# MLP down products with activation tiles in the array and 512-wide weight rows moving

## The chip, the cores and the metric

The kernel runs on one core of a Trainium2 chip. The metric is device time in microseconds for one execution of the whole program; the kernel before takes 2779.71 us (median of 3 runs, 2779.48 to 2797.15).

## What is computed

A two-layer encoder trunk over 256 tokens of width 2048. Layer 0 mixes tokens by sparse attention, layer 1 by an RWKV-7 recurrence; after each comes the MLP that this case is about:

```python
hff = rms_norm(x) * (1 + sc2) + sh2
x = x + g2 * (jnp.square(jax.nn.relu(hff @ mlp_w1[i])) @ mlp_w2[i])
```

`mlp_w1` is 2048 x 8192 and `mlp_w2` 8192 x 2048, float32. A last RMS norm ends the program.

## The kernel before

Activations stand transposed on the chip: `x[f]` is a 128 x 256 tile, 128 features by 256 tokens, 16 tiles in all. Every float32 operand of a product is split into a high part in fp32r and the remainder, and a product is the sum of three matmuls: high times high, high times low, low times high (`acc3`, L179 to L186).

The MLP (`mlp`, L341) goes through the hidden width in four blocks `b` of 2048. For a block, 16 calls of `up(b, f)` (L365) each load one 128 x 2048 slab of `mlp_w1`, run 48 matmuls into one PSUM bank and turn the result into a hidden tile `hid[b, f]` of 128 features by 256 tokens, with its high part in the first 256 columns and its low part in the next 256. Then 16 calls of `down(b, f)` (L382) each load one slab of `mlp_w2`, run 48 matmuls over the 16 hidden tiles into one bank and add the bank into `y[f]` (L389; block 0 copies it, L387). In block 3 each `down` ends by multiplying `y[f]` with its gate and adding it into `x[f]` (L391), then squares `x[f]` for the next norm (`tally`, L290), and GpSimd adds the squares into `ssq` (L292). Two `up` calls of the next block are issued ahead of the down products (`AHEAD_UP`); block 3 has none.

In both kinds of product the weight is the stationary operand: a matmul loads a 128 x 128 weight tile and moves 256 token columns (258 in `up`).

Weights come in pieces of 128 x 512 (`Weights`, L85): SyncE issues a 256 KB load into a ring of 10 raw buffers, ScalarE casts the high part (L92), and the low part is a subtraction (L94), on VectorE for pieces 0 and 1 of a slab and on GpSimd for pieces 2 and 3. High and low parts stand in a ring of 10 pieces; a piece's buffers are free when the last matmul that reads them is done. A slab is four pieces. Beside this the first MLP carries the adaLN rows of the coming layers: at 0.8 rows for each slab, a 1 MB load (L222) and one multiply-and-sum on VectorE (L224); the second MLP carries 0.2 for each slab.

PSUM has two banks each of kinds `d` and `m` and one each of `a` and `b` (asked for as `c`). The products of the MLP take banks in the turn d, c, m (`dense`, L188). The order of instructions on each engine is settled when the program is built, by a scheduler that simulates the engines; each engine then works through its list in order.

Of the kernel before, what the change touches and what calls it, by code (L numbers as in the profile page):

```python
# [7 lines left out]
F32 = mybir.dt.float32  # L8
# [4 lines left out]
OP = mybir.AluOpType  # L13
# [3 lines left out]
P = 128  # L17
D = 2048
S = 256
NS = S + 2  # L20
NF = D // P
# [56 lines left out]
def ada_by_row(layer, part, j):  # L78
    return layer == 1 or part == 5 or (part > 1 and j == 2)
# [22 lines left out]
class Trunk:  # L102
# [238 lines left out]
    def mlp(s, layer):  # L341
        nc = s.nc
        s.kinds = "dcm"


        h = []
        ts = [s.tp.tile([P, 2 * NS], F32R, name="h", bufs=NF) for i in range(NF)]
        rb = s.tp.tile([P, S], F32, name="rb")
        for i, t in enumerate(ts):
            sh = s.m(layer, 3, i).to_broadcast([P, NS - S])  # L350
            nc.gpsimd.tensor_copy(t[:, S:NS], sh)
            nc.gpsimd.tensor_tensor(t[:, NS + S:], sh, t[:, S:NS].bitcast(F32), op=OP.subtract)
        for i, t in enumerate(ts):
            sc = s.m(layer, 4, i)
            nc.scalar.activation(t[:, :S], s.x[i], AF.Copy, scale=sc)
            nc.vector.scalar_tensor_tensor(t[:, NS:NS + S], s.x[i], sc, t[:, :S].bitcast(F32),  # L356
                                           op0=OP.mult, op1=OP.subtract)
            h.append(t)
        for i in range(NF):
            s.tally(i)  # L360
        cols = [k * P for k in range(16)]
        y = [s.tp.tile([P, S], F32, name=f"y{f}") for f in range(NF)]
        hid = {}

        def up(b, f):  # L365
            w = s.wload(s.io["mlp_w1"][layer, b * 16 + f])
            s.ada_due()
            p = s.dense(w, h, cols)
            if b == f == 0:
                nc.scalar.copy(rb, s.rms(D, [s.ssq, s.lsq]))  # L370
            u, r, q = s.B(), s.B(), s.B()
            c = s.small(1)
            nc.scalar.copy(c, p[:, S:S + 1])
            nc.vector.tensor_tensor(u, p[:, :S], rb, op=OP.mult)  # L374
            nc.scalar.activation(r, u, AF.Relu, bias=c)  # L375
            nc.vector.tensor_tensor(q, r, r, op=OP.mult)  # L376
            t = s.O() if 1 < f < 2 + NO else s.A(F32R)
            nc.scalar.activation(t[:, :S], r, AF.Square)
            nc.vector.tensor_tensor(t[:, S:], q, t[:, :S].bitcast(F32), op=OP.subtract)
            hid[b, f] = t  # L380

        def down(b, f):  # L382
            w = s.wload(s.io["mlp_w2"][layer, b, f])
            s.ada_due()
            p = s.dense(w, [hid[b, k] for k in range(16)], cols)
            if b == 0:
                nc.scalar.copy(y[f], p)  # L387
            else:
                nc.vector.tensor_tensor(y[f], p, y[f], op=OP.add)  # L389
            if b == 3:  # L390
                nc.vector.scalar_tensor_tensor(s.x[f], y[f], s.m(layer, 5, f), s.x[f], op0=OP.mult, op1=OP.add)  # L391
                s.tally(f)


        for b in range(4):
            for f in range(AHEAD_UP if b else 0, 16):
                up(b, f)
            for f in range(AHEAD_UP if b < 3 else 0):
                up(b + 1, f)
            for f in range(16):  # L400
                down(b, f)

    def out_group(s, name, layer, block, g, movs, first=0):

# [769 lines left out]
def layout(inputs):  # L1174
    import numpy as np
    g = {k: np.asarray(a) for k, a in inputs.items()}
    f = np.float32
    ct = np.ascontiguousarray
    vec = lambda a: a.reshape(-1, P).T

    def tiles(w, rows, cols):

        n = w.shape[1] // cols
        return ct(w.reshape(rows, P, n, cols).transpose(2, 1, 0, 3)).reshape(n, P, rows * cols)

    a = {}
    a["x"] = ct(g["x"][0].T.reshape(NF, P, S).transpose(1, 0, 2)).reshape(P, NF * S)
    a["positions"] = ct(g["positions"].reshape(-1))
    mu = g["b_mu"][0]
    vs = dict(c=g["c"], final_g=g["final_g"], w0=g["b_w0"], a0=g["b_a0"], k_k=g["b_k_k"], k_a=g["b_k_a"],  # L1190
              gn_g=g["b_gn_g"], gn_b=g["b_gn_b"], r_k=g["b_r_k"], q_norm_g=g["a_q_norm_g"],
              kv_norm_g=g["a_kv_norm_g"], ada_b0=g["ada_b"][0], ada_b1=g["ada_b"][1],
              **{f"mu{i}": mu[i] for i in range(6)})
    a["vec"] = ct(np.concatenate([vec(vs[n]) for n in VEC], 1))
    a["cst"], a["csd"] = constants()
    a["kidx_ln"] = ct(np.stack([g["a_kidx_ln_g"][0], g["a_kidx_ln_b"][0]], 1))
    aw = g["ada_w"]
    rows = aw.transpose(0, 2, 1).reshape(2, 24, 4, P, D)
    cols = aw.reshape(2, 4, 4, P, 24, 512).transpose(0, 4, 1, 3, 2, 5).reshape(2, 24, 4, P, D)
    a["ada_w"] = np.stack([np.stack([(rows if ada_by_row(l, b // 4, b % 4) else cols)[l, b] for b in range(24)])  # L1200
                           for l in range(2)])
    a["c"] = ct(g["c"].reshape(-1))
    a["mlp_w1"] = np.stack([tiles(w, 16, P) for w in g["mlp_w1"]])
    a["mlp_w2"] = np.stack([np.stack([tiles(w[b * 2048:(b + 1) * 2048], 16, P) for b in range(4)])
                            for w in g["mlp_w2"]])
    wi = g["a_w_in"][0]
    a["a_w_in"] = ct(wi[:, :896].reshape(8, 2, P, 896).transpose(0, 2, 1, 3)).reshape(8, P, 1792)
    a["a_w_in_idx"] = tiles(wi[:, 784:912], 16, P)[0]
    a["a_w_qidx"] = tiles(g["a_w_qidx"][0], 4, 512)
    uq = g["a_w_uq"][0].reshape(4, P, 16, 192)  # L1210
    uk = g["a_w_uk"][0].reshape(2, P, 16, P)
    out = []
    for b in range(4):
        hs = range(b * 4, b * 4 + 4)
        parts = [uq[k, :, h, :128] for h in hs for k in range(4)]
        parts += [np.concatenate([uq[k, :, h, 128:], uq[k, :, h + 1, 128:]], 1) for h in hs[::2] for k in range(4)]
        parts += [uk[k, :, h] for h in hs for k in range(2)]
        out.append(np.concatenate(parts[:16], 1))
        out.append(np.concatenate(parts[16:], 1))
    a["a_w_uqk"] = np.stack(out)  # L1220
    uv = g["a_w_uv"][0].reshape(2, P, 2, 2, 512)
    a["a_w_uv"] = ct(uv.transpose(2, 1, 3, 0, 4)).reshape(2, P, 2048)
    for n in ("a_w_o", "b_w_o"):
        w = g[n][0]
        a[n] = np.concatenate([tiles(w[b * 512:(b + 1) * 512], 4, 512) for b in range(4)])
    for n in ("b_w_r", "b_w_k", "b_w_v"):
        a[n] = tiles(g[n][0], 16, P)
    l1 = np.concatenate([g["b_w_w1"][0], g["b_w_a1"][0], g["b_w_g1"][0]], 1)
    a["b_lora1"] = ct(l1.reshape(4, 4, P, 448).transpose(0, 2, 1, 3)).reshape(4, P, 1792)
    l2 = np.zeros((4, P, D), f)  # L1230
    l2[0, :96] = g["b_w_w2"][0]
    l2[1, :96] = g["b_w_a2"][0]
    l2[2:] = g["b_w_g2"][0].reshape(2, P, D)
    a["b_lora2"] = ct(l2.reshape(4, P, NF, P).transpose(2, 1, 0, 3)).reshape(NF, P, 512)
    return a
# [17 lines left out]
```

## Time and profile before

| | |
|---|---|
| runs | 2779.48, 2779.71, 2797.15 us |
| the profiled execution | 2790.62 us, span 2788.7 us |
| mean granted clock of TensorE | 0.963 of full speed |
| TensorE matmuls | 24,884, busy 94% of the span |
| VectorE, ScalarE, GpSimd busy | 70%, 47%, 48% |
| first MLP | about 459 to 1243 us |
| second MLP | about 2037 to 2775 us |

The span is the time from the first to the last instruction. Matmuls overlap, so a single one's duration (283 ns for 256 columns) is longer than the distance from one start to the next, and it is the distance between starts that adds up to time. Idle time of an engine counts only where another waits for it.

### The profile page before, as it was taken

The page shows a single profiled execution, that of the slowest core. Times are in us where ns is not written, and L with a number is a line of the kernel's source. Part 1 is how long each engine was busy: PE and PEld are TensorE (multiplying, and loading weights), DVE is VectorE, ACT ScalarE, POOL GpSimd, SP SyncE. Part 2 cuts the span into 40 slices and gives each one's busy share as a digit, 9 for nine tenths or more (in the row PEclk, how much of TensorE's full clock was granted, in tenths as well). Part 3 has the DMA queues.
Part 4 walks back from the last instruction along what each step waited for, and adds up shares of the span by engine and source line. Part 5 has one row for each costly group of instructions (what it writes and reads, how often), then busy time and mean ns, then how long its engine had stood idle before and what let it go on. Part 6 is the DMA issues. An engine that isn't in the chain of part 4 may idle for free. (4 is left out here: it accounts for less than half of the span.)

```text
span 2788.7 us, 64443 instructions
## 1 busy us (share of the span) xinstructions
PE 2630.8 (94%) x24884; PEld 2446.9 (88%) x24884; DVE 1957.3 (70%) x3183; ACT 1309.4 (47%) x2852; POOL 1345.3 (48%) x1121
## 2 busy tenths in 40 slices
PE   6898998999999999988889999999899999999998
PEld 4566778999999999888888888888799999999998
DVE  2266568998999999968787655666688377473553
ACT  3334435445444444446555343444455455454553
POOL 1243327566577576655655411233465445444444
PEclk9899999999999999999999887999999999999999
DMA  9997745889899898855557522343467767555553
GB/s 370 393 339 270 255 135 187 312 308 348 283 338 328 286 347 311 302 167 152 172 181 246 173 83 75 89 117 97 146 225 219 222 213 243 183 182 184 182 183 115
DMA packets 263620, 624.73 MB, mean 224 GB/s; under 512 B 29328, under 2 KB 43024, under 8 KB 238352
## 3 DMA queue, kind: packets, MB, share of 16 engines
q1 hardware_dynamic: 256400, 608.03, 65.2%
q10 hardware_dynamic: 6912, 12.59, 1.2%
q8 instruction: 195, 3.19, 0.5%
q14 instruction: 113, 0.93, 0.1%
HBM read 603.72 MB, written 16.78 MB: 222 GB/s over the span
## 5 line engine op out<-in xcount | busy, mean ns | idle before, releaser
L94 POOL TENSOR_TENSOR wlo<-raw,whi 128x512 fp32r<-128x512 f32 x364 | 587.1, 1622 | 544.5 <-ACT whi L92 417.2
L92 ACT CAST whi<-raw 128x512 fp32r<-128x512 f32 x856 | 513.0, 619 | 404.7 <-PE ps_d L185 149.1
L94 DVE TENSOR_TENSOR wlo<-raw,whi 128x512 fp32r<-128x512 f32 x492 | 436.5, 892 | 222.6 <-ACT whi L92 211.0
L94 POOL TENSOR_TENSOR wlo<-more,whi 128x512 fp32r<-128x512 f32 x181 | 263.7, 1460 | 322.7 <-ACT whi L92 165.6
L224 DVE CUSTOM_DVE_ANT_0 araw<-araw,cb 128x2048 f32<-128x2048 f32 x124 | 342.6, 2776 | 4.6 <-DMA araw<-ada_w_in 4.6
L184 PE MATMUL ps_d<-A,whi 128*128 128x256 f32 x1058 | 309.4, 293 | 10.6 <-ACT B L863 6.2
L92 ACT CAST whi<-more 128x512 fp32r<-128x512 f32 x366 | 222.0, 618 | 199.0 <-PE ps_d L185 48.5
L185 PE MATMUL ps_d<-A,whi 128*128 128x256 f32 x1058 | 303.5, 287 | 2.3 <-DVE A L198 2.2
L186 PE MATMUL ps_d<-A,wlo 128*128 128x256 f32 x1058 | 303.1, 287 | 0.5 <-DVE wlo L94 0.5
L94 DVE TENSOR_TENSOR wlo<-more,whi 128x512 fp32r<-128x512 f32 (+1 forms) x185 | 174.3, 943 | 138.8 <-ACT whi L92 135.6
L184 PEld LDWEIGHTS ps_d<-A,whi 128*128 128x128 f32 x1058 | 205.4, 195 | 26.2 <-ACT B L863 7.2
L185 PEld LDWEIGHTS ps_d<-A,whi 128*128 128x128 f32 x1058 | 205.5, 194 | 4.8 <-DVE A L198 3.8
L186 PEld LDWEIGHTS ps_d<-A,wlo 128*128 128x128 f32 x1058 | 205.5, 194 | 1.5 <-DVE wlo L94 0.7
L375 ACT ACTIVATE B<-B,sm 128x256 f32<-128x256 f32 x128 | 65.3, 510 | 247.5 <-DVE B L374 247.4
L185 PE MATMUL ps_d<-h,whi 128*128 128x258 f32 x552 | 157.5, 285 | 3.7 <-DVE h L356 3.7
L186 PE MATMUL ps_d<-h,wlo 128*128 128x258 f32 x552 | 155.8, 282 | 2.5 <-DVE wlo L94 2.4
L184 PE MATMUL ps_d<-h,whi 128*128 128x258 f32 x552 | 156.7, 284 | 0.0
L184 PE MATMUL ps_m<-h,whi 128*128 128x258 f32 x540 | 153.4, 284 | 0.0
L185 PE MATMUL ps_m<-h,whi 128*128 128x258 f32 x540 | 153.1, 284 | 0.0
L186 PE MATMUL ps_m<-h,wlo 128*128 128x258 f32 x540 | 152.1, 282 | 0.0
L376 DVE TENSOR_TENSOR B<-B 128x256 f32<-128x256 f32 x128 | 111.5, 871 | 52.9 <-ACT B L375 52.9
L184 PE MATMUL ps_m<-A,whi 128*128 128x256 f32 x506 | 145.1, 287 | 1.1 <-ACT whi L92 1.1
(552 smaller groups left out, 8773.8 us busy)
## 6 DMA issues: line engine op xcount, KB each, us to landing
araw<-ada_w_in SPq DMA_DIRECT2D x192, 1024.0 KB, 7.2
raw<-mlp_w_in SPq DMA_DIRECT2D x614, 256.0 KB, 4.6
more<-mlp_w_in SPq DMA_DIRECT2D x410, 256.0 KB, 4.1
raw<-b_w_r_in SPq DMA_DIRECT2D x64, 256.0 KB, 3.6
raw<-b_w_k_in SPq DMA_DIRECT2D x64, 256.0 KB, 3.8
raw<-b_w_v_in SPq DMA_DIRECT2D x64, 256.0 KB, 3.6
raw<-b_w_o_in SPq DMA_DIRECT2D x64, 256.0 KB, 3.5
hd<-A ACTq DMA_DIRECT2D x48, 256.0 KB, 4.3
```

The lines of the kernel that those rows point to most:

```text
L92: t.nc.scalar.copy(hi[:, :n], r)
L94: e.tensor_tensor(lo[:, :n], r, hi[:, :n].bitcast(F32), op=OP.subtract)
L184: mm(out, wh, m[:, :w], start=i == 0, stop=False)
L185: mm(out, wh, m[:, w:], start=False, stop=False)
L186: mm(out, wl, m[:, :w], start=False, stop=i == n - 1)
L224: nc.vector.tensor_tensor_reduce(out=w, in0=w, in1=s.cb, scale=1.0, scalar=0.0, op0=OP.mult, op1=OP.add, accum_out=acc[:, k:k + 1])
L375: nc.scalar.activation(r, u, AF.Relu, bias=c)
L376: nc.vector.tensor_tensor(q, r, r, op=OP.mult)
```

## The change

The down product is turned round: a 128 x 128 part of a hidden tile (128 hidden features by 128 tokens) is now the stationary operand, and the moving operand is 512 columns of `mlp_w2`. One call `down(b, g)` makes 512 outputs for all 256 tokens, in two banks of the same kind, one for each half of the tokens; there are four calls for a block, and they take the `d` pair and the `m` pair in turn. The sums `y[g][i]` now stand with tokens on partitions and are kept so over all four blocks. Only in block 3 are they turned back: `turn(g)` transposes 128 x 128 pieces on TensorE against the identity, eight for each `g`, and then does the gate, the residual and the square as before. `turn(g - 1)` is called after the first slab of group `g`; `turn(3)` stands after the loop. The stored layout of `mlp_w2` follows; the number and size of the weight pieces stay.

```diff
-        y = [s.tp.tile([P, S], F32, name=f"y{f}") for f in range(NF)]
+        y = [[s.tp.tile([P, 512], F32, name=f"y{g}_{i}") for i in range(2)] for g in range(4)]
...
-        def down(b, f):
-            w = s.wload(s.io["mlp_w2"][layer, b, f])
-            s.ada_due()
-            p = s.dense(w, [hid[b, k] for k in range(16)], cols)
-            if b == 0:
-                nc.scalar.copy(y[f], p)
-            else:
-                nc.vector.tensor_tensor(y[f], p, y[f], op=OP.add)
-            if b == 3:
-                nc.vector.scalar_tensor_tensor(s.x[f], y[f], s.m(layer, 5, f), s.x[f], op0=OP.mult, op1=OP.add)
-                s.tally(f)
+        def down(b, g):
+            kind = "dm"[g % 2]
+            acc = [s.bank(kind) for i in range(2)]
+            for q in range(4):
+                w = s.wload(s.io["mlp_w2"][layer, b, g, q])
+                s.ada_due()
+                for k in range(4):
+                    wh, wl = w.at(k * 512, 512)
+                    n, t = q * 4 + k, hid[b, q * 4 + k]
+                    for i, p in enumerate(acc):
+                        hi, lo = t[:, i * P:(i + 1) * P], t[:, S + i * P:S + (i + 1) * P]
+                        nc.tensor.matmul(p, hi, wh, start=n == 0, stop=False)
+                        nc.tensor.matmul(p, hi, wl, start=False, stop=False)
+                        nc.tensor.matmul(p, lo, wh, start=False, stop=n == 15)
+                if q == 0 and b == 3 and g:
+                    turn(g - 1)
+            for t, p in zip(y[g], acc):
+                if b == 0:
+                    nc.scalar.copy(t, p)
+                else:
+                    nc.vector.tensor_tensor(t, p, t, op=OP.add)
+
+        def turn(g):
+            for o in range(0, 4, 2):
+                p = s.bank("c")
+                for k in range(2):
+                    for i in range(2):
+                        nc.tensor.transpose(p[:, k * S + i * P:k * S + (i + 1) * P], y[g][i][:, (o + k) * P:(o + k + 1) * P],
+                                            s.ident)
+                for k in range(2):
+                    f = g * 4 + o + k
+                    nc.vector.scalar_tensor_tensor(s.x[f], p[:, k * S:(k + 1) * S], s.m(layer, 5, f), s.x[f],
+                                                   op0=OP.mult, op1=OP.add)
+                    s.tally(f)
...
-            for f in range(16):
-                down(b, f)
+            for g in range(4):
+                down(b, g)
+        turn(3)
```

TensorE at the start of the down products of block 1 in the first MLP, before (a tile that ends in `hi` or `lo` is a weight piece, `A` and `o` are hidden tiles; the first name behind the arrow is the operand that moves, the second the one that stands):

```order
L184 MATMUL ps_m_9144<-A_6411,xhi_9120 128x256 [waits Activation_49]
L185 MATMUL ps_m_9144<-A_6411,xhi_9120 128x256
L186 MATMUL ps_m_9144<-A_6411,xlo_9121 128x256 [waits DVE_49]
L184 MATMUL ps_m_9144<-A_6498,xhi_9120 128x256
L185 MATMUL ps_m_9144<-A_6498,xhi_9120 128x256
L186 MATMUL ps_m_9144<-A_6498,xlo_9121 128x256
```

The same place now, at the end of the first run over ten pieces and the start of the second (L395 to L397 are the three matmuls of `down`):

```order
L395 MATMUL ps_d_8712<-whi_8814,A_7925 128x512 [waits Activation_49]
L396 MATMUL ps_d_8712<-wlo_8815,A_7925 128x512 [waits DVE_49]
L397 MATMUL ps_d_8712<-whi_8814,A_7925 128x512
L395 MATMUL ps_d_8712<-xhi_8820,A_8013 128x512 [waits Activation_49]
L396 MATMUL ps_d_8712<-xlo_8821,A_8013 128x512 [waits DVE_49]
L397 MATMUL ps_d_8712<-xhi_8820,A_8013 128x512
L395 MATMUL ps_d_8713<-xhi_8714,A_6403 128x512 [waits DVE_49]
L396 MATMUL ps_d_8713<-xlo_8715,A_6403 128x512
L397 MATMUL ps_d_8713<-xhi_8714,A_6403 128x512
```

The list of TensorE now takes 30 matmuls into one bank, through ten different pieces, before the first into the other bank, which comes back to the first piece; such runs stand at the start of block 1 (30 matmuls), block 2 (20) and block 3 (29) of the first MLP, and of two blocks of the second (30 and 27). Elsewhere the two banks alternate every three matmuls.

VectorE at the end of the second MLP, before (`y` are the sums, `x` the residual tiles, L266 is the first step of the last norm):

```order
L389 TENSOR_TENSOR y13_27874<-ps_d_37910,y13_27874 128x256
L391 SCALAR_TENSOR_TENSOR x13_79<-y13_27874,mod1_85,x13_79 128x256
L389 TENSOR_TENSOR y14_27875<-ps_b_37988,y14_27875 128x256
L391 SCALAR_TENSOR_TENSOR x14_80<-y14_27875,mod1_85,x14_80 128x256
L389 TENSOR_TENSOR y15_27876<-ps_m_38066,y15_27876 128x256
L391 SCALAR_TENSOR_TENSOR x15_81<-y15_27876,mod1_85,x15_81 128x256
L266 TENSOR_SCALAR sm_38123<-ps_m_38118 128x2
```

The same place now (L404 adds a bank into the sums, L416 is the gate and residual):

```order
L404 TENSOR_TENSOR y3_0_26299<-ps_m_34736,y3_0_26299 128x512
L404 TENSOR_TENSOR y3_1_26300<-ps_m_34737,y3_1_26300 128x512
L416 SCALAR_TENSOR_TENSOR x12_78<-ps_a_34958,mod1_85,x12_78 128x256
L416 SCALAR_TENSOR_TENSOR x13_79<-ps_a_34958,mod1_85,x13_79 128x256
L416 SCALAR_TENSOR_TENSOR x14_80<-ps_b_34971,mod1_85,x14_80 128x256
L416 SCALAR_TENSOR_TENSOR x15_81<-ps_b_34971,mod1_85,x15_81 128x256
L266 TENSOR_SCALAR sm_34987<-ps_m_34982 128x2
```

Before, one tile's sum and residual stand behind the last matmul; now two additions of 512 columns, eight transposes on TensorE between them and L416, and four residuals do.

## Rows read from the trace of the kernel before

**Rows 1.** The page, busy time of the engines over the span.

```profile
PE 2630.8 (94%) x24884; PEld 2446.9 (88%) x24884; DVE 1957.3 (70%) x3183; ACT 1309.4 (47%) x2852; POOL 1345.3 (48%) x1121
```

**Rows 2.** Busy time by stage, first MLP: down 1, up 2, down 2, down 3.

```profile
core 0: us, PE busy (x) PEld busy (x) DVE busy (x) ACT busy (x) POOL busy (x), PEclk, DMA share, GB/s
...
772.00:868.00 96.00, 94.13 (x772) 93.93 (x771) 94.79 (x93) 44.63 (x78) 71.78 (x35) 0.98 0.97 341
868.00:961.00 93.00, 92.90 (x771) 92.69 (x770) 86.09 (x95) 43.81 (x99) 51.35 (x30) 1.00 0.89 301
961.00:1059.00 98.00, 94.29 (x772) 94.01 (x771) 96.47 (x92) 44.24 (x77) 68.24 (x35) 0.98 0.92 333
...
1140.00:1243.00 103.00, 95.72 (x776) 95.14 (x774) 78.91 (x95) 46.60 (x91) 65.53 (x45) 0.95 0.70 230
```

**Rows 3.** Busy time by stage, second MLP: down 2 and up 3 (columns as above).

```profile
2511.00:2603.00 92.00, 92.00 (x769) 92.00 (x768) 31.61 (x52) 40.53 (x66) 41.48 (x32) 1.00 0.57 184
2603.00:2683.00 80.00, 80.00 (x666) 80.00 (x666) 55.25 (x67) 45.21 (x95) 36.20 (x28) 1.00 0.60 183
```

**Rows 4.** Timeline of TensorE (start, length), first matmuls of two down products that follow each other.

```profile
643.63 0.28 PE L184 MATMUL ps_b<-A,whi 128*128 128x256 f32 x1
...
649.39 0.28 PE L184 MATMUL ps_m<-A,whi 128*128 128x256 f32 x1
```

**Rows 5.** Timeline of TensorE, matmuls of 512 moving weight columns in layer 0's attention.

```profile
230.66 0.39 PE L590 MATMUL ps_d<-whi,A 128*128 128x512 f32 x1
...
232.28 0.39 PE L591 MATMUL ps_d<-wlo,A 128*128 128x512 f32 x1
...
235.90 0.39 PE L592 MATMUL ps_d<-whi,A 128*128 128x512 f32 x1
```

**Rows 6.** Timeline of TensorE around two transposes (L1080) in the recurrence.

```profile
1715.93 0.44 PE L1080 MATMUL ps_m<-cst,fin 128*128 128x128 f32 x2
1716.13 0.36 PE L185 MATMUL ps_d<-xv,whi 128*128 128x256 f32 x1
1716.33 0.28 PE L186 MATMUL ps_d<-xv,wlo 128*128 128x256 f32 x1
```

**Rows 7.** Durations on VectorE, ns shortest/median/longest, by tile.

```profile
L389 DVE TENSOR_TENSOR y<-ps_m,y x33: 409/424/426, 791.6 to 2775.2; 128x256 f32<-128x256 f32 x33
L391 DVE SCALAR_TENSOR_TENSOR x<-y,mod,x x32: 472/485/1515, 1162.7 to 2775.7; 128x256 f32<-128x256 f32 x32
L94 DVE TENSOR_TENSOR wlo<-raw,whi x492: 649/692/1825, 24.6 to 2753.0; 128x512 fp32r<-128x512 f32 x162, 128x256 fp32r<-128x256 f32 x2
```

**Rows 8.** Waits of TensorE in the first MLP (us in total, times, longest).

```profile
PE ps_b L184 <- ACT A L378: 5.3, 1, 5.3
PE ps_d L186 <- DVE wlo L94: 5.3, 3, 2.2
PE ps_m L186 <- DVE wlo L94: 3.7, 1, 3.7
```

**Rows 9.** Timeline of all engines at the end of the second MLP.

```profile
2774.89 0.28 PE L186 MATMUL ps_m<-A,xlo 128*128 128x256 f32 x1
...
2775.21 0.42 DVE L389 TENSOR_TENSOR y<-ps_m,y 128x256 f32<-128x256 f32 x1 [4.82 <-PE ps_m L186]
2775.67 0.48 DVE L391 SCALAR_TENSOR_TENSOR x<-y,mod,x 128x256 f32<-128x256 f32 x1
2776.19 0.42 ACT L290 ACTIVATE lsq<-x 128x256 f32<-128x256 f32 x1 [5.34 <-DVE x L391]
2776.66 0.38 PE L306 MATMUL ps_m<-cst,lsq 128*128 128x1 f32 x2 [1.37 <-ACT lsq L290]
...
2777.53 0.16 DVE L266 TENSOR_SCALAR sm<-ps_m 128x2 f32<-128x2 f32 x1 [1.37 <-PE ps_m L306]
```

**Rows 10.** Timeline, GpSimd adding one tile's squares.

```profile
2759.47 0.74 POOL L292 TENSOR_TENSOR ssq<-ssq,B 128x256 f32<-128x256 f32 x1 [2.51 <-DVE wlo L94]
```

**Rows 11.** Timeline at the end of the first MLP: last matmul, first of the next stage.

```profile
1242.21 0.28 PE L186 MATMUL ps_a<-A,wlo 128*128 128x256 f32 x1
...
1251.44 0.58 PE L184 MATMUL ps_d<-A,whi 128*128 128x256 f32 x1 [3.94 <-ACT A L197]
```

More of the change, by code (lines that the diff above doesn't have):

```diff
@@ L1203, in layout @@
     a["mlp_w1"] = np.stack([tiles(w, 16, P) for w in g["mlp_w1"]])
-    a["mlp_w2"] = np.stack([np.stack([tiles(w[b * 2048:(b + 1) * 2048], 16, P) for b in range(4)])
-                            for w in g["mlp_w2"]])
+    a["mlp_w2"] = ct(g["mlp_w2"].reshape(2, 4, 4, 4, P, 4, 512).transpose(0, 1, 5, 2, 4, 3, 6)).reshape(2, 4, 4, 4, P, 2048)
     wi = g["a_w_in"][0]
```

## The prediction

> **What bounds the kernel now.** The page comes first: TensorE is busy for 94% of the span and VectorE for 70% [rows 1], so TensorE is the engine to look at, and a mean over the span says no more. The busy time by stage comes next. In the second MLP TensorE is busy for all of 92 us and all of 80 us, at a granted clock of 1.00, with VectorE at 32 and 55 us [rows 3]: there every ns taken from a matmul is a ns of the program. The first MLP looks different. TensorE is nearly full there too, but VectorE is busy for 94.8 of 96, 86.1 of 93 and 96.5 of 98 us [rows 2], since it carries the adaLN rows, and TensorE's waits name it: matmuls on a low part that VectorE had not finished, 5.3 and 3.7 us, and 5.3 us for a hidden tile at the start of block 3 [rows 8]. Two engines are near their limit there, and a faster TensorE may run into the other.
>
> The third view is the timeline, for the distance between starts. A down product of 48 matmuls of 256 columns goes from 643.63 to 649.39 [rows 4]: 5.76 us, or 120.0 ns for each. At the clock of 2.4 GHz that the stage shows, 256 columns are 106.7 ns, so each matmul costs 13.3 ns more than its columns.
>
> **The stream of down products.** Before, 2 layers x 4 blocks x 16 x 48 = 6,144 matmuls of 256 columns; after, 2 x 4 x 4 x 96 = 3,072 of 512. The columns are the same; the question is what one of 512 costs. The attention stage has this very form, weight columns moving past an activation tile: from 232.28 to 235.90 there are 16 distances, 226.3 ns each; from 230.66 there are 23, 227.8 each [rows 5]. I take 227.0. Then 6,144 x 120.0 = 737.3 us become 3,072 x 227.0 = 697.3: 40.0 us less, 20.0 in each MLP (42.1 at 226.3, 37.5 at 227.8). This says that the 13 ns belong to the matmul and not to its columns.
>
> The Trainium skill has another rule: "TensorE: Matmul & The Clock Gate", section "Back-to-back issue gap", gives columns over clock and 2.5 ns for a warm matmul by itself. By it a pair would shrink only by 2.5 ns and 3,072 pairs by 7.7 us. The trace does not agree, with 13.3 ns at 256 columns; this is rival E below.
>
> **Transposes within block 3.** Six of the eight turns stand inside the stream. Two transposes take 0.20 us to the start of the next matmul, and that one's successor starts 0.20 instead of 0.12 us later [rows 6]: 0.20 to 0.28 us for two, 0.8 to 1.1 us for the eight of a turn. I take 1.0, or 6.0 us in all. They wait for the additions into `y`, but 24 matmuls of the next group stand ahead of them, 5.4 us of cover for two additions.
>
> An addition of 512 columns from PSUM is not in the trace. One of 256 takes 0.42 us, and a 512-column subtraction 0.69 [rows 7]; it lies between 0.42 and 0.85, and I take 0.69. In the second MLP the cover holds. In the first VectorE runs late and what waits behind a transpose is all of TensorE: 0 to 6 us, of which I take 2.
>
> The skill's same page, section "Part 4: PE-mode transpose", gives some 275 ns for a transpose in a kernel. At that price 48 transposes would be an estimated 13 us, and the sum 7 us worse. The trace's pair in 0.20 to 0.28 us disagrees and decides.
>
> **The two ends.** Behind the last matmul stood one addition (0.42), one residual (0.48), one square (0.42): the last norm's matmul on it starts at 2776.66, 1.49 us after the last product ended at 2775.17, and its sums are read at 2777.53, 2.36 us after [rows 9]. Now the first bank is done three matmuls early, so its addition ends about with the stream; the second ends at 0.75. Transposes through the array: to 1.3. Four residuals of 0.48 with gaps: 1.35 to 3.35. The squares follow each; but three of the four tiles are also added on GpSimd, one behind the other at 0.74 [rows 10]: 2.35, 3.1, 3.85, 4.6. Four short matmuls follow, some 1.1 us: the sums are read at 5.75, 3.4 us later than before. Lower bound 2 us, if the additions on GpSimd overlapped fully with the residuals; upper bound 6. The first MLP ends alike, with TensorE waiting from 1242.5 to 1251.4 [rows 11], so 3.4 there too: 6.8 us.
>
> **VectorE in the first MLP.** It has 16 additions of 0.42 for a block less (6.7 us) and 8 of 0.69 more (5.5), a relief of 1.2 us. TensorE saves 5.0 us for a block. In the stretch of block 1's down products and of block 2, VectorE is busy for 277.4 of 287 us [rows 2]; ahead of a waiting matmul on a low part, most of what TensorE gains it then waits for. Up products lose the lead over TensorE that down products build. So of the 10 us of blocks 1 and 2 I count 6 as lost again (bounds: 0 and 10). Block 0 starts with a full lead and block 3 ends with the adaLN rows done (78.9 of 103 us busy, same rows): nothing lost there.
>
> The runs of 20 to 30 matmuls into one bank at the start of three blocks ask for a piece every 0.68 us, twice the mean rate. What is late then is made up by the second run, which needs no new piece; I cost them at nothing while that holds, and up to 6 us each if it does not.
>
> **Block 3's stall.** TensorE waited 5.3 us for a hidden tile of the last `up` [rows 8], with the clock of that stage down to 0.95 [rows 2]. Before, the first down product needed the last hidden tile 5.6 us after the down products began; now its group lasts 21.8 us and needs it after at least 13. The wait should go; what is late next is a low part, so I take 5 of the 5.3 us and the 2 or 3 of clock (bounds 0 and 9).
>
> DMAs do not change: as many pieces, 256 KB each, in the same queue.
>
> **The sum.** 40.0 - 6.0 - 2.0 - 6.8 - 6.0 + 5.0 = 24 us less. The profiled execution would go from 2790.6 to 2766.6. It was 10.9 us above the median of the runs; I take the same step from the median: 2779.7 - 24 = 2756 us, or 0.9% faster. A measurement of this kernel can tell about 1% (28 us) from no change. The likeliest case's own range is 2746 to 2766.
>
> **Rivals.**
> B, VectorE keeps up: nothing is lost in blocks 1 and 2, no transpose waits, and the stall of block 3 goes with its clock: 40 - 6 - 6.8 + 9 = 36 us, 2744. For it speaks that VectorE's busy time in the down stages includes waiting on GpSimd (the longest subtraction is 1.8 us against a median of 0.69 [rows 7]), against it rows 8.
> C, the first MLP gives nothing: VectorE bounds it, and all 20 us there turn into waits on low parts: 20 - 6 - 6.8 = 7 us, 2773. Rows 2 speak for it, block 3's free VectorE against it.
> D, slower: in the first MLP the runs into one bank use up all ten pieces, whose buffers come free only in the second run. Through a first run VectorE stands with a full ring, 6.8, 4.5 and 6.6 us for 30, 20 and 29 matmuls, on an engine that has no slack: 18 us on top of C, 11 us slower, 2791. It decides from the point where VectorE fills the ring well before the run ends; but pieces come at 1.4 us and are asked for at 0.68, so the ring should be empty rather than full.
> E, the 13 ns are no cost of a matmul: 7.7 - 6 - 6.8 = 5 us slower, 2785. Only if rows 5 are special.
>
> **How the numbers follow.** Forecast 0.48, B 0.25, C 0.18, D 0.06, E 0.03. The scheduler also reorders the stages that follow, which I count at nothing, give or take 6 us. Faster by over 1% (under 2752) is B with 8 of the forecast's 48 in 100: 0.33. Slower by over 1% (over 2807) would be D with more than its price and the reordering against it: 0.04. The rest, 0.63, is within 1%. The range 2738 to 2778 holds the forecast, most of B and of C.
>
> **What would show it.** Right: down matmuls of the second MLP 227 ns apart and that MLP 17 us shorter up to its last product; the last norm's sums read some 5.8 us after the last product; eight transposes in about 1.0 us; more waits on low parts in blocks 1 and 2 of the first MLP, no wait for a hidden tile in block 3. Wrong: a distance of 213 or 240 ns, waits of TensorE on the transposes' additions of several us, or a first MLP as long as before.

## The result and the profile after

The changed kernel takes 2750.98 us (median of 4 runs, 2750.90 to 2751.64), the kernel before 2779.6 us on the same chip (4 runs, 2771.6 to 2797.15). The ratio is 0.988, 95% interval 0.9855 to 0.9906: 28.6 us less. The forecast was 2756, with a range of 2738 to 2778.

The profiled executions stand at 2751.64 and 2790.62 us, 39.0 us apart. By the starts of TensorE's matmuls, the 39 us lie in these stretches:

| stretch (us) | before | after | difference | forecast |
|---|---|---|---|---|
| up to the first MLP's first product | 460.9 | 459.4 | -1.5 | 0 |
| first MLP, first to last product | 781.3 | 773.7 | -7.6 | -14 |
| last product to last norm matmul, first MLP | 2.35 | 7.13 | +4.8 | +3.4 |
| norm, project, scan, first up stage of the second MLP | 895.6 | 871.2 | -24.3 | 0 |
| second MLP from there to its last product | 634.8 | 619.3 | -15.5 | -17 |
| last product to last norm matmul, second MLP | 2.35 | 6.73 | +4.4 | +3.4 |

The rows of the turned products add up to -14 us, not to the -24 of the sum. A stretch that the change does not touch gives the other 24 us. It is called the untouched stretch below, and four of the twelve experiments are about it (e1, e2, e8, e9).

The page of after answers to [rows 1]: fewer matmuls, the same share of busy time.

```profile
PE 2587.6 (94%) x21876; PEld 2282.0 (83%) x21876; DVE 1946.8 (71%) x3135; ACT 1312.8 (48%) x2836; POOL 1344.8 (49%) x1121
```

First the products themselves. The timeline of TensorE in the second MLP, first matmul of one group and first of the next [rows 4, 5]:

```profile
2473.13 0.40 PE L395 MATMUL ps_d<-whi,A 128*128 128x512 f32 x1
...
2494.91 0.39 PE L395 MATMUL ps_m<-whi,A 128*128 128x512 f32 x1
```

96 matmuls in 21.78 us are 226.9 ns each; 227.0 was forecast. Busy time by stage for the same down products and the up products behind them (columns as in [rows 2]; [rows 3] are the stages of before):

```profile
2473.00:2560.00 87.00, 87.00 (x387) 72.09 (x386) 28.06 (x42) 40.67 (x67) 41.23 (x32) 1.00 0.58 193
2560.00:2641.00 81.00, 81.00 (x673) 80.96 (x672) 56.05 (x70) 45.71 (x95) 36.33 (x28) 1.00 0.57 184
```

The down stage went from 92 to 87 us, TensorE still full at a granted clock of 1.00, and the up stage did not change (81.0 us in both by the starts of its matmuls; the windows are cut to whole us).

A turn in block 3 of the second MLP, eight transposes between products [rows 6]:

```profile
2668.18 0.39 PE L397 MATMUL ps_m<-whi,o 128*128 128x512 f32 x1
2668.41 0.60 PE L412 MATMUL ps_a<-cst,y 128*128 128x128 f32 x4
2668.84 0.60 PE L412 MATMUL ps_b<-cst,y 128*128 128x128 f32 x4
2669.20 0.48 PE L395 MATMUL ps_m<-whi,o 128*128 128x512 f32 x1
2669.51 0.40 PE L396 MATMUL ps_m<-wlo,o 128*128 128x512 f32 x1
```

From 2668.41 to 2669.20 are 0.79 us, and the next distance is 0.31 instead of 0.23: 0.87 us for a turn. Each waits for additions (ns, shortest/median/longest) that take what was taken for them, 0.69 us [rows 7]:

```profile
L404 DVE TENSOR_TENSOR y<-ps_d,y x24: 673/680/692, 804.8 to 2709.0; 128x512 f32<-128x512 f32 x24
L404 DVE TENSOR_TENSOR y<-ps_m,y x24: 672/684/692, 826.3 to 2731.1; 128x512 f32<-128x512 f32 x24
```

The first MLP is another matter. Busy time by stage of down 1, up 2, down 2 and down 3 [rows 2]:

```profile
772.00:868.00 96.00, 92.20 (x422) 75.75 (x421) 93.94 (x82) 44.61 (x75) 73.16 (x36) 1.00 0.94 337
868.00:961.00 93.00, 91.26 (x737) 90.68 (x735) 84.45 (x97) 44.08 (x102) 52.52 (x30) 0.98 0.86 302
961.00:1059.00 98.00, 91.98 (x411) 76.32 (x410) 96.14 (x84) 44.30 (x75) 69.30 (x36) 0.97 0.95 345
...
1140.00:1243.00 103.00, 92.84 (x412) 76.17 (x412) 74.81 (x108) 47.57 (x85) 65.49 (x44) 0.95 0.67 227
```

VectorE is as full as before. TensorE's waits on low parts (`wlo`, `xlo`), first MLP [rows 8]:

```profile
PE ps_d L396 <- DVE wlo L94: 11.7, 3, 6.0
PE ps_m L186 <- DVE wlo L94: 3.7, 1, 3.7
...
PE ps_d L395 <- DVE B L375: 3.5, 1, 3.5
PE ps_a L186 <- DVE wlo L94: 3.4, 1, 3.4
```

With four smaller ones the waits on low parts are 23.2 us; the same list of before adds up to 14.0. The 3.5 us are of another kind: at the start of block 0's down products the first group waits for a bank that VectorE has yet to empty (L375). The wait of 5.3 us for a hidden tile in block 3 is gone, but at the same place stands one for a low part. The timeline there shows why, and what it costs behind itself:

```profile
1137.11 4.66 POOL L94 TENSOR_TENSOR wlo<-raw,whi 128x512 fp32r<-128x512 f32 x2 [0.32 <-ACT whi L92]
...
1137.26 3.39 DVE L224 CUSTOM_DVE_ANT_0 araw<-araw,cb 128x2048 f32<-128x2048 f32 x1
...
1139.27 0.39 PE L395 MATMUL ps_d<-whi,o 128*128 128x512 f32 x1
...
1140.58 3.34 DVE L224 CUSTOM_DVE_ANT_0 araw<-araw,cb 128x2048 f32<-128x2048 f32 x1
...
1143.85 0.68 DVE L94 TENSOR_TENSOR wlo<-raw,whi 128x512 fp32r<-128x512 f32 x1
...
1144.58 0.59 PE L396 MATMUL ps_d<-wlo,o 128*128 128x512 f32 x1 [4.92 <-DVE wlo L94]
...
1144.97 0.63 PE L397 MATMUL ps_d<-whi,o 128*128 128x512 f32 x1
...
1145.40 0.63 PE L395 MATMUL ps_d<-whi,A 128*128 128x512 f32 x1
```

Two adaLN rows stand one behind the other on VectorE, ahead of the subtraction that TensorE needs. Before had the same pair at this place, ahead of the step (L374) from which the hidden tile is made:

```profile
1142.38 3.39 DVE L224 CUSTOM_DVE_ANT_0 araw<-araw,cb 128x2048 f32<-128x2048 f32 x1
...
1145.70 3.34 DVE L224 CUSTOM_DVE_ANT_0 araw<-araw,cb 128x2048 f32<-128x2048 f32 x1
...
1149.57 0.41 DVE L374 TENSOR_TENSOR B<-ps_m,rb 128x256 f32<-128x256 f32 x1
...
1151.03 0.58 PE L184 MATMUL ps_b<-A,whi 128*128 128x256 f32 x1 [5.33 <-ACT A L378]
```

So it is VectorE that is late there, whatever TensorE happens to need first. Each of after's five longest waits inside the first MLP, the one for the bank included, ends 0.7 to 1.0 us after such a pair (they end at 550.7, 583.9, 759.1, 968.8 and 1144.6). A version that keeps the rows apart was not run.

When the wait is over, matmuls come 0.43 us apart instead of 0.227: TensorE runs at the lower of its two clocks (1.2 instead of 2.4 GHz). All distances between starts in the first MLP can be sorted by their length. At the undisturbed distance (227 ns for 512 columns, 120 for 256, 109 for a transpose) they would take 738.7 us before and 721.0 after. Distances 1.45 to 2.6 times as long, the slow clock, add 9.8 and 14.8 us; longer ones, the waits, add 31.5 and 36.5 (1.4 us is jitter in both). So the products gave 17.7 us, transposes included, and waits and slow clock took 5.0 each. By block the first MLP became shorter by 4.7, -0.2, -1.3 and 4.5 us: blocks 0 and 3 gained, blocks 1 and 2 together (381.3 us before, 382.8 now) gained nothing.

The end of the second MLP [rows 9, 10]:

```profile
2730.45 1.37 DVE L404 TENSOR_TENSOR y<-ps_m,y 128x512 f32<-128x512 f32 x2 [13.83 <-PE ps_m L397]
...
2730.70 0.39 PE L397 MATMUL ps_m<-xhi,A 128*128 128x512 f32 x1
...
2733.26 0.86 DVE L416 SCALAR_TENSOR_TENSOR x<-ps_b,mod,x 128x256 f32<-128x256 f32 x2
2733.54 2.33 POOL L292 TENSOR_TENSOR ssq<-ssq,B 128x256 f32<-128x256 f32 x3 [12.42 <-ACT B L290]
...
2735.92 0.59 PE L306 MATMUL ps_m<-cst,ssq 128*128 128x1 f32 x2 [3.17 <-POOL ssq L292]
2736.37 0.57 PE L306 MATMUL ps_m<-cst,lsq 128*128 128x1 f32 x2
2736.80 0.57 PE L306 MATMUL ps_m<-cst,ssq 128*128 128x1 f32 x2
2737.22 0.57 PE L306 MATMUL ps_m<-cst,lsq 128*128 128x1 f32 x2
2737.83 0.16 DVE L266 TENSOR_SCALAR sm<-ps_m 128x2 f32<-128x2 f32 x1 [3.70 <-PE ps_m L306]
```

GpSimd's three additions end at 2735.87, 4.8 us after the last product's end at 2731.09 (4.6 forecast). The four norm matmuls behind them come 0.43 us apart; before, they started at 2776.66, 2776.91 and 2777.13, 0.22 to 0.25 apart. The sums are read 6.7 us after the last product.

### The profile page after: what moved, and what is told of

It reads as the page before. It is cut to its first block, busy times and chain, and to the rows that moved or that the text cites. A ratio compares the mean times of both kernels' runs of the same rounds, so it can differ in the third digit from the quotient of the medians.

```text
span 2749.5 us, 58296 instructions
## 1 busy us (share of the span) xinstructions
PE 2587.6 (94%) x21876; PEld 2282.0 (83%) x21876; DVE 1946.8 (71%) x3135; ACT 1312.8 (48%) x2836; POOL 1344.8 (49%) x1121
## 5 line engine op out<-in xcount | busy, mean ns | idle before, releaser
L94 DVE TENSOR_TENSOR wlo<-raw,whi 128x512 fp32r<-128x512 f32 x492 | 443.0, 908 | 206.4 <-ACT whi L92 200.2
L224 DVE CUSTOM_DVE_ANT_0 araw<-araw,cb 128x2048 f32<-128x2048 f32 x124 | 335.7, 2720 | 5.6 <-DMA araw<-ada_w_in 5.5
L94 DVE TENSOR_TENSOR wlo<-more,whi 128x512 fp32r<-128x512 f32 (+1 forms) x185 | 168.4, 912 | 116.6 <-ACT whi L92 112.8
L184 PE MATMUL ps_d<-A,whi 128*128 128x256 f32 x656 | 197.9, 303 | 7.8 <-ACT B L890 4.0
L185 PE MATMUL ps_d<-A,whi 128*128 128x256 f32 x656 | 191.6, 293 | 4.0 <-DVE A L198 3.7
L186 PE MATMUL ps_d<-A,wlo 128*128 128x256 f32 x656 | 190.5, 291 | 0.0
L184 PEld LDWEIGHTS ps_d<-A,whi 128*128 128x128 f32 x656 | 129.9, 199 | 23.3 <-issue 5.0
L185 PEld LDWEIGHTS ps_d<-A,whi 128*128 128x128 f32 x656 | 129.9, 198 | 7.5 <-DVE A L198 6.1
L186 PEld LDWEIGHTS ps_d<-A,wlo 128*128 128x128 f32 x656 | 129.7, 198 | 0.7 <-issue 0.5
L395 PE MATMUL ps_d<-whi,A 128*128 128x512 f32 x300 | 118.4, 395 | 3.9 <-DVE B L375 3.5
```

The source lines that it names most:

```text
L94: e.tensor_tensor(lo[:, :n], r, hi[:, :n].bitcast(F32), op=OP.subtract)
L184: mm(out, wh, m[:, :w], start=i == 0, stop=False)
L185: mm(out, wh, m[:, w:], start=False, stop=False)
L186: mm(out, wl, m[:, :w], start=False, stop=i == n - 1)
L224: nc.vector.tensor_tensor_reduce(out=w, in0=w, in1=s.cb, scale=1.0, scalar=0.0, op0=OP.mult, op1=OP.add, accum_out=acc[:, k:k + 1])
L395: nc.tensor.matmul(p, hi, wh, start=n == 0, stop=False)
```

## The experiments

Theories: the turned products are worth their 5 us per block where nothing else bounds, and in the first MLP VectorE takes much of it back. The untouched stretch became shorter because its instructions stand in another order. Rivals: the DMA queues bound the first MLP; the runs into one bank do; the untouched stretch only varies from one execution to the next. "Stretch" in the table is the untouched one, "second MLP" goes from its first up stage's end to its last product; both and the first MLP are from the profiled execution.

| run | whole, median | ratio to before [95%] | first MLP | stretch | second MLP |
|---|---|---|---|---|---|
| before / after | 2779.6 / 2751.0 | 0.988 [0.9855, 0.9906] | 781.3 / 773.7 | 895.6 / 871.2 | 634.8 / 619.3 |
| e1 second MLP alone | 2778.0 | 0.9974 [0.9955, 0.9993] | 781.5 | 886.6 | 623.1 |
| e2 first MLP alone | 2769.1 | 0.9934 [0.9909, 0.9958] | 774.9 | 877.9 | 634.8 |
| e3 after, short rows | 2710.9 | 0.9731 [0.9701, 0.9760] | 732.7 | 869.3 | 619.4 |
| e4 before, short rows | 2753.0 | 0.9870 [0.9840, 0.9899] | 750.7 | 889.0 | 634.8 |
| e5 after, squares | 2740.3 | 0.9856 [0.9824, 0.9888] | 762.9 | 869.2 | 620.2 |
| e6 after, banks | 2743.1 | 0.9858 [0.9834, 0.9883] | 771.1 | 867.8 | 617.0 |
| e7 both | 2737.8 | 0.9838 [0.9816, 0.9860] | 760.9 | 875.3 | 616.9 |
| e8 before, late end | 2776.1 | 0.9979 [0.9959, 0.9999] | 777.9 | 883.3 | 634.8 |
| e9 after, late end | 2761.1 | 0.9903 [0.9874, 0.9933] | 771.8 | 879.4 | 619.2 |
| e10 e7 and rate | 2747.5 | 0.9861 [0.9835, 0.9887] | 771.1 | 871.6 | 617.8 |
| e11 e10 and end | 2744.6 | 0.9838 [0.9805, 0.9872] | 772.2 | 871.9 | 618.7 |
| e12 before, squares, rate | 2781.3 | 0.9985 [0.9965, 1.0004] | 777.2 | 902.8 | 634.8 |

Before's median was 2785.2 us beside e1 to e4, 2781.1 beside e5 to e8, 2786.5 beside e9 to e12.

**One MLP at a time.** e1 keeps the old product in layer 0, e2 in layer 1:

```diff
+        turned = layer in (1,)
...
-            for g in range(4):
+            for g in range(4) if turned else []:
                 down(b, g)
-        turn(3)
+            for f in [] if turned else range(16):
+                down_f(b, f)
+        if turned:
+            turn(3)
```

> Down products turned in the second MLP alone; the first MLP is that of before. The project and scan stages between the MLPs keep the instruction order of before on every engine. Theory (that stretch became 24 us shorter because the schedule of these untouched stages is another one): the stretch from the first MLP's norm to the end of the second MLP's first up stage takes 885 to 896 us as before, the second MLP's rest 619 instead of 635 us, its end 4.4 us more: 2779.6 - 15.5 + 4.4 = 2768 us. Rival (the 24 us are a difference between two executions and have nothing to do with the order): the stretch falls anywhere between 871 and 896 us.

> Down products turned in the first MLP alone; the second MLP is that of before. Project and scan have the instruction order of after. Theory (the order of the untouched stages made the 24 us): the stretch takes 871 us within 3, the first MLP 774, and the whole 2751 + 15.5 - 4.4 = 2762 us. Rival (differences between executions): the stretch falls anywhere between 871 and 896 us, and the change of the first MLP alone is worth 7.6 - 4.7 = 3 us: 2777 us.

With the products turned in the second MLP alone the untouched stretch stays long, 886.6; with the first alone it is short, 877.9. In e1 the whole falls by 7.2 us, and its own parts give that without any rest: the second MLP 11.7 less, its end 4.4 more (after has 15.5 there; e1's first down stage has waits of 3.2 and 0.8 us for low parts and takes 93.2 us, where after's takes 87.1). In e2 the whole falls by 16.1, where its own parts give 6.4 - 4.8 = 1.6. Both wholes are above what the theory gave, 2768 and 2762, but before too was 5.6 us slower beside them than beside after; as differences, 7.2 and 16.1 us stand against 11 and 18 from the theory. e2's stretch is above its 871 within 3. The place is right; the size, 24 us, was taken from one execution and is too large: e2's whole leaves 16.1 - 1.6 = 14.5 us for it.

**VectorE or DMA.** e3 and e4 leave out three quarters of each adaLN sum on VectorE in the first MLP, in after and in before, so that a row takes 0.67 us at the shortest instead of 2.27:

```diff
-                nc.vector.tensor_tensor_reduce(out=w, in0=w, in1=s.cb, scale=1.0,
+                n = 512 if s.rate == 0.8 else D
+                nc.vector.tensor_tensor_reduce(out=w[:, :n], in0=w[:, :n], in1=s.cb[:, :n], scale=1.0,
```

> The kernel after, with each adaLN row of the first MLP multiplied and summed over its first 512 columns only (three quarters of that sum are left out); all loads stay. Theory (VectorE with the adaLN rows is what bounds the first MLP): TensorE's waits on low parts there fall from 23 us to under 4, the first MLP from 774 to 755 us or less, the whole to about 2732 us. Rival (the DMA queues, 94 to 96% busy in the down stages, make the pieces late): waits and time of the first MLP stay within 4 us of 774, the whole at 2748 to 2751.

> The kernel before, with the same three quarters of the adaLN sum left out in the first MLP; all loads stay. Theory (VectorE): the waits on low parts go from 14 us to under 3, the first MLP from 781 to about 768 us, so that with VectorE relieved the turned products are worth 13 to 17 us in the first MLP instead of 7.6. Rival (DMA): the first MLP stays at 778 to 781 us and the pair stays 7 to 8 us apart.

No wait on a low part is left in the first MLP of either, which falls to 732.7 and 750.7 us: 18.0 apart, where the full kernels are 7.6 apart. Busy time from one block's up products to the next's, block 1 to 2, of e3 and of e4:

```profile
843.00:1023.00 180.00, 180.00 (x1155) 165.00 (x1154) 107.33 (x177) 92.87 (x176) 83.93 (x64) 1.00 0.93 335
```

```profile
854.00:1039.00 185.00, 185.00 (x1540) 185.00 (x1540) 109.86 (x188) 93.04 (x176) 83.52 (x64) 1.00 0.93 329
```

A block takes 180 instead of 185 us, 5.0 less as forecast, with TensorE full and the DMA engines 93% busy in both: the DMA rival falls. The gain was larger than expected (2711 instead of 2732 us): sorted as above, the waits of all kinds fall from 36.5 to 7.2 us, where 19 us had been forecast for those on low parts, and the slow clock behind them from 14.8 to 3.4.

**A version with less on VectorE, and the runs into one bank.**

```diff
-            nc.vector.tensor_tensor(q, r, r, op=OP.mult)
+            nc.scalar.activation(q, r, AF.Square)
```

> The kernel after, with the 64 products r times r of the up tiles (0.70 us each on VectorE, 45 us in the first MLP) computed by ScalarE as squares. Theory (VectorE bounds the first MLP): it does 45 us less there, so the 23 us of TensorE's waits on low parts fall to 5 to 12, the first MLP from 774 to about 756 us, the second stays, the whole goes from 2751 to about 2733 us. Rival (the lateness is in the chain cast, subtraction, and more work on ScalarE delays casts as much): first MLP 770 us or more, the whole at 2747 to 2755.

```diff
             for f in range(AHEAD_UP if b else 0, 16):
+                s.kinds = "dcm" if f < 12 else "cm"
                 up(b, f)
```

> The kernel after, in which the last four up products of a block and the two ahead stay off the d banks, so that the first down group finds both its banks free; the list of TensorE then holds no run into one bank longer than 24. Theory (the runs take pieces twice as fast as they are made, when VectorE is already late): the waits at the start of the down products, some 18 us in the first MLP, fall by 8 or more, the first MLP comes to 766 us or less, the second loses its 2.4 us, the whole goes to about 2741 us. Rival (VectorE's mean rate bounds the first MLP, a wait that goes returns later): first MLP within 3 us of 774, only the 2.4 us of the second gained: about 2748 us.

> Both edits together on the kernel after. If the two act on different causes (VectorE's amount of work, the runs into one bank), the first MLP falls to about 750 us and the whole to about 2727 us; if the runs cost nothing by themselves, it equals the version with the squares alone within 3 us in the first MLP.

The squares on ScalarE take 10.8 us off the first MLP, less than the 18 expected: the waits on low parts fall from 23.2 to 16.6 us, not below 12. Without the runs into one bank at the starts of the blocks the first MLP is 2.6 us shorter, which its own variation covers in part (773.7, 774.9 and 771.8 in the three kernels with the same code for it), and the second 2.3 us. Beside the squares the bank edit is worth 2.0 us in the first MLP: the runs hardly count by themselves, as the rival said. e7, with 2737.8 us, is the fastest of those that leave nothing out. It was not run beside after, but the kernel before took nearly the same beside each (2781.1 and 2779.6).

**The order of the untouched stretch.** Extra operations at the end of the first MLP make the scheduler put the stages behind it in yet another order:

```diff
                 nc.vector.tensor_tensor(y[f], p, y[f], op=OP.add)
+                for _ in range(2 if layer == 0 and b == 3 and f == 15 else 0):
+                    nc.vector.tensor_tensor(y[f], y[f], y[f], op=OP.max)
```

> The kernel before, where the last output tile of the first MLP passes two more VectorE operations that leave it as it is (max with itself, 0.4 us each), so that the first MLP ends about 1 us later. The scheduler then gives project and scan an order close to that of after (GpSimd's lists agree for 97%, TensorE's for 78%). Theory (the order of those stages made most of the unforeseen gain): the stretch from the norm to the end of the second MLP's first up stage takes 870 to 880 us instead of 887 to 896, the whole 2765 to 2772 us although no product is turned. Rival (the turned products themselves or the chip's state shorten it): the stretch stays at 886 us or more.

```diff
                     nc.vector.scalar_tensor_tensor(s.x[f], p[:, k * S:(k + 1) * S], s.m(layer, 5, f), s.x[f],
                                                    op0=OP.mult, op1=OP.add)
+                    for _ in range(4 if layer == 0 and f == 15 else 0):
+                        nc.vector.tensor_tensor(s.x[f], s.x[f], s.x[f], op=OP.max)
```

> The kernel after, where the last residual tile of the first MLP passes four more VectorE operations that leave it as it is (some 1.7 us). Project and scan get an order unlike both before (TensorE 57% alike) and after (64%). Theory (their time follows the order): the stretch from the norm to the end of the second MLP's first up stage moves by more than 4 us away from the 868 to 878 us of the kernels with after's order, in either direction, and the whole with it. Rival (the turned products, or what they leave behind, shorten it): it stays within 868 to 880 us and the whole at 2751 to 2755.

Neither decides. e8's 883.3 us lie between what the theory and the rival said; e9's 879.4 are within the rival's bounds, while its whole, 2761, is above them; but before was 6.9 us slower beside e9 than beside after, and the intervals of the two ratios (0.990 and 0.988) overlap. What the fourteen profiles do show is where the stretch differs. "Missing" is the time that the lower clock took away: one minus the granted clock, summed over the scan from its first matmul to its last transpose.

| kernels, by the order of these stages | project | scan | missing | scan less missing |
|---|---|---|---|---|
| before | 328.3 | 436.6 | 35.7 | 400.9 |
| e12, before's order | 329.3 | 442.9 | 45.6 | 397.3 |
| e1 and e4, before's order | 328.9, 327.8 | 427.1, 429.8 | 25.8, 28.9 | 401.3, 400.9 |
| e8, e9, two other orders | 325.4, 326.9 | 428.3, 421.2 | 23.1, 16.1 | 405.2, 405.1 |
| after | 324.0 | 415.7 | 15.0 | 400.7 |
| seven others with after's order | 322.1 to 328.3 | 412.2 to 422.7 | 9.8 to 23.8 | 398.9 to 402.4 |

Three windows from the scan's start, of before, of e12 and of after:

```profile
1573.00:1645.00 72.00, 69.34 (x1438) 58.83 (x1438) 37.31 (x118) 24.31 (x67) 8.59 (x7) 0.83 0.34 99
1645.00:1717.00 72.00, 71.47 (x1109) 59.93 (x1100) 39.71 (x121) 26.55 (x76) 13.01 (x13) 0.73 0.23 68
1717.00:1789.00 72.00, 71.01 (x1374) 59.97 (x1373) 49.97 (x140) 30.74 (x87) 17.83 (x17) 0.95 0.29 82
```

```profile
1575.00:1647.00 72.00, 69.76 (x1311) 59.23 (x1313) 33.76 (x106) 22.40 (x61) 7.55 (x6) 0.76 0.32 95
1647.00:1719.00 72.00, 71.43 (x1141) 59.87 (x1138) 41.97 (x128) 26.51 (x76) 14.02 (x14) 0.71 0.23 68
1719.00:1791.00 72.00, 71.12 (x1384) 59.86 (x1383) 46.12 (x134) 28.29 (x83) 13.91 (x14) 0.91 0.26 76
```

```profile
1564.00:1636.00 72.00, 69.09 (x1535) 58.78 (x1536) 41.92 (x128) 26.46 (x75) 10.17 (x9) 0.88 0.29 94
1636.00:1708.00 72.00, 71.83 (x1313) 61.17 (x1311) 46.62 (x144) 29.70 (x84) 14.94 (x15) 0.93 0.29 89
1708.00:1780.00 72.00, 71.46 (x1451) 60.76 (x1447) 51.06 (x148) 31.69 (x89) 17.48 (x17) 1.00 0.30 96
```

TensorE is busy for 69 to 72 us of each window in all three. What differs is the granted clock, the number before the last two, and with it the matmuls that a window holds. With the missing clock taken off, what is left is the same within some 5 us: 397 to 401 us in before's order, 399 to 402 in after's. Of these two orders neither costs the scan more by itself (e8's and e9's cost some 5 us); what separates the two groups is the clock. Before, e1, e4 and e12 have one order in common, and yet their scans differ by 16 us.

**Three misses.** e10 is e7 with the first edit below, e11 is e10 with the second (the loops over `k` and `i` become one over `each`), and e12 is before with the squares of e5 and the first edit.

```diff
-        t.rate = 0.8
+        t.rate = 0.76
...
+                each = [(k, i) for k in range(4) for i in range(2)]
+                if b == g == q == 3:
+                    each = [(k, i) for i in range(2) for k in range(4)]
```

> The version with squares on ScalarE and the free d banks, and 0.76 adaLN rows for each slab in the first MLP instead of 0.8, so that they last to its end. Theory (VectorE's amount of work in the stages that wait): 1.8 us less VectorE work in a stage of 16 slabs, the first MLP from 761 to about 755 us, the whole to about 2731 us. Rival (the waits come from two rows that stand one behind the other on VectorE, whatever their rate): first MLP 760 to 762 us, the whole as before at 2737.

> As the version with 0.76 rows, and in the very last slab of an MLP the first bank takes its four pieces before the second does, so that its addition (0.69 us) lies beside the second bank's products. Theory (the two additions stand in the chain of the end): from the last product to the last norm matmul 6.0 us instead of 6.7 in the second MLP and 6.4 instead of 7.1 in the first, 1.4 us in all. Rival (GpSimd's additions of squares set the end): both ends as long as before.

> The kernel before with the same relief of VectorE (squares on ScalarE, 0.76 rows). Theory (VectorE hid part of the turned products' worth): its waits on low parts fall from 14 to under 5 us, the first MLP from 781 to 768 to 771 us, some 13 us above the turned version with the same relief instead of 7.6; project and scan have before's order, so that stretch takes 885 to 896 us and the whole 2768 to 2775. Rival (the relief works as much in both): first MLP 762 to 765 us.

In e10 the first MLP is 10.2 us longer than in e7, not shorter, and 7.5 of it lie in block 3's down products (94.4 to 101.9 us): they now carry 12 adaLN rows, the last at 1197 us, instead of 7, the last at 1168, and TensorE's waits there, for low parts and for additions ahead of the transposes, go from 2.1 to 7.9 us. In e11 both ends are as in e10 (7.13 and 6.02 us). The end of the second MLP in e10 shows that nothing was to be had:

```profile
2725.87 1.37 DVE L404 TENSOR_TENSOR y<-ps_m,y 128x512 f32<-128x512 f32 x2 [13.83 <-PE ps_m L397]
...
2726.12 0.39 PE L397 MATMUL ps_m<-xhi,A 128*128 128x512 f32 x1
...
2731.34 0.38 PE L306 MATMUL ps_m<-cst,ssq 128*128 128x1 f32 x2 [3.17 <-POOL ssq L292]
2731.58 0.36 PE L306 MATMUL ps_m<-cst,lsq 128*128 128x1 f32 x2
...
2732.43 0.16 DVE L266 TENSOR_SCALAR sm<-ps_m 128x2 f32<-128x2 f32 x1 [2.89 <-PE ps_m L306]
```

The first addition begins before the last product ends and is hidden already. The norm matmuls are 0.24 us apart here and 0.43 in after, behind the same wait of 3.17 us: the end is 0.7 us shorter for the clock alone. e12 gained 4 us in the first MLP where 10 to 13 were expected, and the pair e10 and e12 is 6.1 us apart there, no more than the pair without the relief. (Both hold the rate that harmed e10, and e10 alone the bank edit; before with the squares alone was not run.) So a moderate relief of VectorE does not show the products' worth; only e3 and e4, with the waits gone, do.

## Why the prediction was right, and where it was not

The time lies 5 us under the forecast and inside the likeliest case's own range, but that it lies so near is luck. By the terms of the sum the change was worth 14 us, not 24, which gives 2766; the rest came from stages that the sum counted at nothing. By 1 us the time also falls among those under 2752, which had a chance of 0.33, and not into the 0.63 within 1%.

- *The stream, 40.0.* Right: 226.9 ns where 227.0 was taken, 5.0 us per block in e3 against e4. Rival E falls: 512 columns are 213.3 ns at 2.4 GHz, so 13.6 ns are left, about as many as for 256 columns. By the Trainium skill ("TensorE: Matmul & The Clock Gate", section "Back-to-back issue gap", columns over clock and 2.5 ns for a matmul by itself) an estimated 215.8 ns would stand there; the trace does not agree.
- *Transposes within block 3, 6.0 and 2.0.* Right in kind: 0.87 us each, 5.2 for six, and 0.9 us of waits on the additions. A single transpose lasts 273 ns (median of L412), near the 275 that the Trainium skill gives in the same page's section "Part 4: PE-mode transpose", but eight of them start within 0.79 us.
- *The two ends, 6.8.* Mis-sized: 9.2. GpSimd's chain came as worked out (4.8 us for 4.6). The four short matmuls, 1.1 us in the sum, took 1.9, since they ran at the lower clock behind the wait; in e10, at the higher, the sums are read 5.9 us after the last product, for the 5.75 forecast.
- *VectorE, 6.0, and block 3's stall, +5.0.* That VectorE takes much of the gain back was right, both sizes were not. Blocks 1 and 2 lost all of their 10 us, the upper bound, where 6 were taken (they take 379.6 us in e1 and in e8, with before's first MLP, and 382.7 and 379.7 in e2 and e9, with after's). In block 3 the hidden tile's wait went, and a low part's wait of 4.9 us took its place, which the prediction named and priced at 0.3: it took the tile for what was late, and it was VectorE behind its pair of rows. Waits added 5.0 us over the whole MLP and the slow clock behind them another 5.0, a term that the sum did not have for new waits. The first MLP gave 7.6 us up to its last product instead of 14. Rival C, that it gives nothing, came nearer than rival B.
- *The runs into one bank, 0.* At most some 2 us in each MLP by e6; rival D's 18 us are nowhere.
- *The stages that follow, 0 give or take 6.* This step failed. They gave 24.3 us between the profiled executions. Before's lay 11.0 us above the median of its runs. If that excess lies in this stretch (the profiled executions of e1 and e4, within 2 us of their medians, have 886.6 and 889.0), 13 us are left; with 14 for the products and ends and 1.5 ahead of the first product they make the 28.6 us between the medians. e2's whole gives much the same, 14.5.

That the gain of these stages follows from turning the first MLP is shown by e1 and e2, and that most of it is granted clock in the scan by the table and the windows. That the order of the instructions is what lowers the clock was argued only: every kernel with before's order has a longer stretch (886.6 to 902.8 us) than any with after's (867.8 to 877.9), but e8 and e9 left it open. Each of these is one execution besides: e4's own runs lie between 2743.8 and 2754.9 us, the profiled one is the longest of them, and so the ranges of the two orders may well meet.

## What to carry to other kernels

Where a trace holds the same kind of matmul at two widths, the distances of both give the cost per instruction, and a wider form can be priced to the ns. On a stretch where a second engine is nearly full, price the wait that takes the place of the one removed, and with it the slow clock behind it; e3's form of run (shorten one engine's work and look whether the waits go) tells the second bound apart. Look also at what stands ahead of a late instruction on its engine: here long rows that came in pairs mattered, and the engine's mean share of busy time did not show them. When the order is settled by a scheduler, turn one part of the change at a time before the whole gain is put down to the change: here as much came from stages that nobody touched.

## What the runs showed of the hardware

Behind a wait of 4.9 us matmuls of 512 columns came 0.43 us apart, at the lower clock, before 0.227 returned; all of the waits of 3.4 us or more in after's first MLP had slow distances behind them. It is not so each time: behind the same wait of 3.17 us the last norm's matmuls ran at the lower clock in after and at the higher in e10. VectorE and GpSimd stretch each other: an adaLN row takes 2.27 us at the shortest (half of the 96 at most 2.29) and 3.39 while two subtractions run on GpSimd, and those take 4.66 us for the two, where a single one takes 1.29:

```profile
L224 DVE CUSTOM_DVE_ANT_0 araw<-araw,cb x96: 2274/2292/3418, 482.7 to 1178.0; 128x2048 f32<-128x2048 f32 x96
```

```profile
959.71 1.29 POOL L94 TENSOR_TENSOR wlo<-raw,whi 128x512 fp32r<-128x512 f32 x1 [2.47 <-DMA more<-mlp_w_in]
```

And one and the same order of the scan took 427 to 443 us, mostly by the clock granted in its first 216 us.
